# A decoder layer on one core: attention's last value products moved into the next step, and one right-hand operand built one product later

## The chip, the cores and the metric

The kernel runs on one core of one Trainium2 chip. A core has a matrix engine (TensorE, called PE in the profile, with a second row PEld for its weight loads), three engines for elementwise work (VectorE or DVE, ScalarE or ACT, GpSimd or POOL), an engine whose queue here only issues transfers (SyncE or SP), and 16 DMA engines. Each engine takes its instructions in the order in which they stand in its own queue. The metric is the time of one run on the device in microseconds (us). Before the change it is 2248.29 us, the median of 3 runs that lie between 2247.93 and 2248.32 us.

## The reference

One layer for 1024 rows of width 1024, in float32:

```
x = x + 0.5 * swiglu(rms_norm(x), ffn1 weights)            # ffn1, hidden width 2816
h = rms_norm(x)
fq, fk, fv, f_logit, sq, sk, sv, g_fox, g_sb = split(h @ w_in)
y_fox = forgetting_attention(...)     # 8 heads of 64: causal softmax of q.k plus summed log forget gates
y_sb  = stick_breaking_attention(...) # 8 heads of 64: sigmoid(z) times the product of (1 - sigmoid(z)) behind it
x = x + (sigmoid(g_fox) * (y_fox @ w_branch_fox) + sigmoid(g_sb) * (y_sb @ w_branch_sb)) @ w_out
x = x + 0.5 * swiglu(rms_norm(x), ffn2 weights)            # ffn2
x = x + sigmoid(rms_norm(x) @ w_ple_gate) * (p @ w_ple_proj)   # per-layer input embedding, "ple"
```

Here `swiglu(h) = (silu(h @ w_gate) * (h @ w_up)) @ w_down`.

## The kernel before, in words

**Precision.** Every float32 factor is split into two parts that TensorE takes in its faster format: the high part is a rounding copy on ScalarE (a "CAST" row of the profile), the low part is the difference, a subtraction on VectorE (a "TENSOR_TENSOR" row on the same tile). A product is the sum of high by high, high by low and low by high: 12 matmuls of 128x512 for four blocks of the inner dimension.

**The up products.** The gate and up projections of both feed-forward stages, the two gate projections of the mixer and ple's gate projection all go through `make_up`. It computes a 256-column piece n of a weight matrix against the 1024 rows with seven products m = 1 to 7 of sums and differences of quarters instead of eight plain ones. `B[m]` is the right-hand operand of product m, made from the activations; it serves all pieces n of the stage. The last to be made is `B[4]`, in four parts j = 0 to 3: `combo_d(j)` forms the difference on VectorE (two instructions in ffn1, L731 and L732; elsewhere one, L734), and `combo_e(j)` writes its high part (ScalarE, L649) and its low part (VectorE, L653). `begin(s)` issues them behind the s-th product of the stage, in the order of `up_order`: (n, m) = (2,1), (1,5), (2,2), (1,6), (2,6), (1,7), (2,5), (1,3), (2,7), (1,4), and then seven for each further n. So (1,4), the tenth, is the first to read `B[4]`. ffn1 has a form of its own (`rows()`): there its parts are 128 columns of all four inner blocks, so that the first matmul of a product needs all four parts; elsewhere a part is one inner block, and only the fourth matmul of (1,4) needs part 3. `evict` takes a finished product out of its bank; for m = 7 that is a copy on ScalarE, an addition on VectorE and, where n is a gate piece, an activation on ScalarE. The weights are loaded by SyncE's queue into `raw` slots and split by `prep` four products ahead. All of this is issued in exactly the order in which the program writes it.

**Attention.** A step is one head and a quarter c of the rows (256 rows). `scores` makes two rows of blocks (128 rows each) of the scores of a step, one at each resumption; `apply` takes the step before the last, transposes its weights in groups of 256 keys (`transposes`: TensorE into a bank "pt", then a high copy on ScalarE L1212 and a low subtraction on VectorE L1218), and multiplies them with the values (`values`, L1236). `values(0)` is the last product of a step; ScalarE then copies one half of the bank "av" (L1262), and the function `add`, kept in the list `late` until the next `flush`, adds the other half on VectorE (L1265). At the end of a pair of heads `add` also splits y into two parts (ScalarE L1271, VectorE L1272) and sends them to `y_pairs` by two transfers of SyncE. "sc" has three banks, "pt" two and "av" one. `fill` puts projection work of later heads between these pieces. A scheduler sets the order here, but TensorE keeps the written order, and in the stick-breaking heads VectorE and ScalarE keep it too for the operations that are marked with `order`.

**Start and end.** In the first 12 us `busy(count)` issues matmuls whose result nobody reads (L253). At the end, ple's gate (1024 columns in four pieces) is multiplied with a product of p, x is added, and the result is stored. For the last row blocks x is fetched into a tile (`fetch(..., True)`) and added on VectorE; for the first ones x is added by a transfer that accumulates into the tile (L1720, issued by GpSimd). `AT` lists behind which product each of these stands: `fetch` loads, `finish` multiplies and adds, `store` writes a tile out.

Of the kernel before, what the change touches and what calls it, by code (L numbers as in the profile page):

```python
# [18 lines left out]
P = 128  # L19
# [17 lines left out]
def tile_hybrid_decoder_layer(  # L37
# [51 lines left out]
    def f(ap):  # L89
        return ap.bitcast(F32)  # L90
# [434 lines left out]
    def up_order(nm_):  # L525

        seqn = [(2, 1), (1, 5), (2, 2), (1, 6), (2, 6), (1, 7), (2, 5), (1, 3), (2, 7), (1, 4)]
        for n in range(3, nm_ - 1):
            seqn += [(n, 1), (n - 1, 4), (n, 2), (n - 1, 3), (n, 6), (n, 5), (n, 7)]
        n = nm_ - 1  # L530
        return seqn + [(n, 1), (n - 1, 4), (n, 2), (n, 6), (n, 5), (n, 7), (n - 1, 3), (n, 3), (n, 4)]

    def make_up(N, src, nm_, tags, first_fn, first_done=None, over=None):
# [50 lines left out]
        def last_sum(n, eng=nc.gpsimd):  # L584
            eng.tensor_sub(part(n, 2), part(n, 2), part(n, 6))
# [46 lines left out]
        def rows():  # L632
            return "rows" in N[0]
# [108 lines left out]
        def begin(s):  # L742

            if s == 0:
                sums(2, nc.vector, True)
            elif s == 1:
                for q in range(4):
                    combo_s(q, 7)
            elif s == 2:
                last_sum(1, nc.vector)  # L750
            elif s == 3:
                third_sum(2, nc.vector)
            elif s == 7:
                last_sum(2, nc.vector)
            for j in range(4):
                if s == (j + 2 if rows() else 2 + j // 2):
                    combo_d(j)
            if 3 < s < 8:
                combo_e(s - 4)
        return types.SimpleNamespace(a=combo_a, b=combo_b, t=combo_t, l=combo_l, u=combo_u, s=combo_s, load=load, prep=prep, sums=sums, last_sum=last_sum, plain=plain, silu=silu, product=product, begin=begin, E=E, B=B, bank_of=bank_of)  # L760

    def ffn(N, wg, wu, wd, resid, hid, tags, entry, tail):
# [5 lines left out]
        seqn = up_order(nm_)  # L768
# [3 lines left out]
        def evict(n, m, ps):  # L772
            up, j = n % 2, n // 2
            if m == 1:
                E[n] = [slot(t, [P, 2, 512]) for t in (("GF", "RN"), ("Y", "Y"))[up]]
# [348 lines left out]

    def flush():
        while late:
            late.pop(0)()
# [67 lines left out]
    def apply(step, fill):  # L1195
# [3 lines left out]
        av = bank("av")  # L1199
# [23 lines left out]
        def values(kpair):  # L1223
            pt = pts[kpair]
            mm = []
# [32 lines left out]
        values(0)  # L1258
# [3 lines left out]
        nc.scalar.copy(ys, av[HD:P, :256])  # L1262

        def add():
            ins = nc.vector.tensor_add(ys, av[0:HD, :256], ys)  # L1265
            if not step["fox"]:
                order("dve", ins)
            if hh == 1 and c % 2 and not step["last"]:
                cs = slice(c // 2 * 512, c // 2 * 512 + 512)
                hi = slot("PT", [P, 512], F32R)  # L1270
                a = nc.scalar.copy(hi[:], Y["t"][:, cs])  # L1271
                b = nc.vector.tensor_sub(Y["t"][:, cs].bitcast(F32R), Y["t"][:, cs], f(hi[:]))  # L1272
                if not step["fox"]:
                    order("act", a)
                    order("dve", b)
                nc.sync.dma_start(yd[Y["idx"], 0][:, cs], f(hi[:]))
                nc.sync.dma_start(yd[Y["idx"], 1][:, cs], Y["t"][:, cs])
        late.append(add)
# [82 lines left out]
    def attention():  # L1361
# [73 lines left out]
        for h in range(16):  # L1435
# [20 lines left out]
            for c in range(4):  # L1456
# [7 lines left out]
                next(rows)  # L1464
                run(islice(turns, (1, 2, 1, 1)[c]))
# [5 lines left out]
        for step in prev:  # L1471
            run(apply(step, lambda: run(islice(rest, 6))))
        flush()
# [49 lines left out]
    def first_entry(F):  # L1523
# [14 lines left out]
        busy(6)  # L1538
# [12 lines left out]
        busy(4)  # L1551
# [62 lines left out]
    tags = {"raw": {1: ("KH", "KL")}, "sum": {}, "w": ("Q", "Q", "KH", "KL"), "hl": ("WL", "WL", "WL", "WH") + ("PT",) * 4 + ("WL", "WL", "WL", "PT"), "B": {"12": "X", 3: ("T",) * 4, 5: "H", 6: "H", 7: "X", 4: "X"}}  # L1614
# [90 lines left out]
    def ple_start():  # L1705
# [26 lines left out]
        def evict(n, m, ps):  # L1732
# [19 lines left out]
            elif m == 4:  # L1752
# [4 lines left out]
              9: [(fetch, 3, 0, "T")], 10: [(finish, 1, 0)], 11: [(finish, 1, 1), (fetch, 3, 1, "Q"), (store, 0, 0)], 12: [(store, 0, 1), (fetch, 3, 1, "GF", True)],  # L1757
# [61 lines left out]
```

## Time and profile before

| what | value |
|---|---|
| median of 3 runs | 2248.29 us |
| the profiled execution's own time | 2247.58 us |
| span of its trace | 2245.8 us |
| busy: PE, PEld | 2216.0 us (99%), 1881.5 us (84%) |
| busy: DVE, ACT, POOL | 1510.8 us (67%), 1006.0 us (45%), 820.5 us (37%) |
| DMA, mean over the span | 133 GB/s |

The span runs from the first to the last record of the trace; the profiled execution's own time is 1.8 us longer. The busy shares are averages over stages with different limits. The stages, by the lines of their matmuls, lie at: ffn1's entry 0 to 70 us, its up products to 446, its down products to 638, the entry of the gates to 706, gates, values, queries and keys to 850, attention to 1381, branches and output projection to 1500, ffn2's entry to 1567, its up products to 1942 and down products to 2133, ple's entry to 2205, and the end.

### The profile page before, as it was taken

How to read it: one execution, taken by the hardware profiler on the slowest of the kernel's cores; microseconds unless marked ns; L12 is line 12 of the kernel's file. 1: busy time of each engine (PE TensorE's matmuls, PEld its weight loads, DVE VectorE, ACT ScalarE, POOL GpSimd, SP SyncE). 2: the span in 40 equal slices, each digit the busy share in tenths (PEclk: the TensorE clock that was granted, in tenths of full speed). 3: DMA queues.
4: the chain of work that ended last, by engine and by line, in shares of the span. 5: the costliest groups of instructions: out<-in, count | busy, mean ns of one | idle time of the engine just before them, and what ended most of it. 6: DMA issues, size and time to landing. Idle time of an engine off the chain costs nothing.

```text
span 2245.8 us, 30545 instructions
## 1 busy us (share of the span) xinstructions
PE 2216.0 (99%) x11216; PEld 1881.5 (84%) x11216; DVE 1510.8 (67%) x2366; ACT 1006.0 (45%) x1805; POOL 820.5 (37%) x787
## 2 busy tenths in 40 slices
PE   9999999999999999999999999999999999999998
PEld 7788888888888899999898888888888888888886
DVE  8754555598887324666678885889555554778897
ACT  6433333433455435555566663255333333333454
POOL 2353544210021336556566663520544354200111
PEclk9999999999999999999999999999999999999999
DMA  3332323394322334233324466741423232655327
GB/s 132 100 130 80 131 80 131 111 348 168 119 94 97 129 107 129 85 104 86 85 53 100 112 202 214 255 158 49 141 84 128 80 132 80 234 215 192 115 92 225
DMA packets 196183, 298.04 MB, mean 133 GB/s; under 512 B 28729, under 2 KB 108857, under 8 KB 196034
## 3 DMA queue, kind: packets, MB, share of 16 engines
q1 hardware_dynamic: 195312, 293.47, 39.6%
q0 software_dynamic: 720, 2.62, 0.6%
q8 instruction: 88, 1.44, 0.3%
q14 instruction: 61, 0.50, 0.1%
q10 hardware_dynamic: 2, 0.00, 0.0%
HBM read 196.14 MB, written 83.13 MB: 124 GB/s over the span
## 4 chain that ended last, share of the span: by engine, by line
PE 85%; DVE 10%; ACT 2%; issue 1%; DMA 1%; POOL 0%; DVEq 0%; ACTq 0%; POOLq 0%
PE ps L617 37%; PE ps L509 22%; PE ps L895 8%; PE ps L903 5%; PE ps L1498 4%; PE ps L1236 3%; PE ps L1210 2%; PE ps L1152 1%; PE ps L1151 1%; PE ps L561 1%; PE ps L1057 1%; DVE PT L1218 1%; DVE RN L1114 1%; DVE GF L1114 1%; DVE WL L106 1%
## 5 line engine op out<-in xcount | busy, mean ns | idle before, releaser
L509 PE MATMUL ps<-H,H 128*128 128x512 f32 x2184 | 497.3, 389 | 0.0
L509 PEld LDWEIGHTS ps<-H,H 128*128 128x128 f32 x2184 | 409.5, 188 | 84.9
L617 PE MATMUL ps<-H,WL 128*128 128x512 f32 x1176 | 278.3, 389 | 1.5 <-DVE Y L783 0.5
L617 PEld LDWEIGHTS ps<-H,WL 128*128 128x128 f32 x1176 | 220.5, 188 | 48.4 <-DVE Y L783 0.9
L185 POOL TENSOR_TENSOR PT<-PT,PT 128x512 f32<-128x512 f32 x27 | 34.9, 1294 | 403.9 <-ACT PT L182 403.0
L617 PE MATMUL ps<-H,Q 128*128 128x512 f32 x624 | 148.4, 389 | 0.0
L517 DVE SCALAR_TENSOR_TENSOR X<-ps,X 128x512 f32<-128x512 f32 x168 | 110.2, 685 | 47.4 <-PE ps L509 47.3
L617 PE MATMUL ps<-X,WL 128*128 128x512 f32 (+1 forms) x576 | 136.8, 387 | 4.4 <-ACT KH L1780 4.4
L617 PEld LDWEIGHTS ps<-H,Q 128*128 128x128 f32 x624 | 117.1, 188 | 24.3
L617 PEld LDWEIGHTS ps<-X,WL 128*128 128x128 f32 x576 | 107.6, 190 | 26.3 <-ACT KH L1780 4.6
L617 PE MATMUL ps<-H,PT 128*128 128x512 f32 x528 | 125.8, 389 | 0.0
L139 POOL TENSOR_TENSOR WL<-RAW,WH 128x512 fp32r<-128x512 f32 (+1 forms) x84 | 98.6, 1195 | 68.0 <-ACT WH L129 43.6
L1218 DVE TENSOR_TENSOR PT<-ps,PT 128x512 fp32r<-128x512 f32 (+1 forms) x160 | 100.0, 627 | 30.0 <-ACT PT L1212 29.2
L895 PE MATMUL ps<-WH,H 128*128 128x256 f32 x768 | 116.1, 287 | 0.8 <-ACT RN L960 0.8
L617 PEld LDWEIGHTS ps<-H,PT 128*128 128x128 f32 x528 | 99.0, 188 | 20.6
L903 PE MATMUL ps<-H,WH 128*128 128x512 f32 x384 | 115.0, 406 | 0.0
L1236 PE MATMUL ps<-PT,X 128*128 128x256 f32 (+1 forms) x640 | 102.3, 286 | 6.4 <-DVE PT L1218 5.5
L1212 ACT CAST PT<-ps 128x512 fp32r<-128x512 f32 (+1 forms) x160 | 87.1, 548 | 42.5 <-PE ps L1210 41.3
L1236 PEld LDWEIGHTS ps<-PT,X 128*128 128x128 f32 x640 | 90.2, 190 | 16.7 <-DVE PT L1218 10.2
L895 PEld LDWEIGHTS ps<-WH,H 128*128 128x128 f32 x768 | 101.4, 190 | 2.7 <-ACT RN L960 1.3
L412 POOL TENSOR_TENSOR PT<-GF,RN 128x512 f32<-128x512 f32 x20 | 33.7, 1686 | 190.8 <-DVE GF L803 190.8
L1164 POOL TENSOR_TENSOR T<-T,l 128x128 f32<-128x128 f32 (+3 forms) x64 | 73.3, 1148 | 71.8 <-DVE l L1163 69.8
(447 smaller groups left out, 4790.0 us busy)
## 6 DMA issues: line engine op xcount, KB each, us to landing
hidden<-PT SPq DMA_DIRECT2D x40, 512.0 KB, 2.7
WH<-in_ffn_w_gate_dram SPq DMA_DIRECT2D x38, 512.0 KB, 4.7
Q<-hidden SPq DMA_DIRECT2D x24, 512.0 KB, 6.3
hidden<-RN SPq DMA_DIRECT2D x22, 512.0 KB, 2.6
KH<-in_ffn_w_up_dram SPq DMA_DIRECT2D x20, 512.0 KB, 6.2
KL<-in_ffn_w_up_dram SPq DMA_DIRECT2D x20, 512.0 KB, 6.9
T<-in_ffn_w_down_dram SPq DMA_DIRECT2D x20, 512.0 KB, 6.2
GF<-hidden SPq DMA_DIRECT2D x14, 512.0 KB, 7.6
```

Source lines behind the costliest of these rows:

```text
L139: ins = eng_lo.tensor_sub(lo[part], raw[part], f(hi[part]))
L509: pe(nc.tensor.matmul(groups[g][t][:], wt[:, b, k, t * P:(t + 1) * P], act[:, a, k, :], start=(fresh and n == 0), stop=(i in (6, 1, 4) and ...
L517: nc.vector.scalar_tensor_tensor(xs, groups[g][t][:], scale, xs, ALU.mult, ALU.add)
L617: pe(nc.tensor.matmul(ps[:, cols], hl[:, a, k, :], right(B[m], b, k)[:, cols], start=(first and i == 0), stop=(final and i == 11), skip_gr ...
L895: pe(nc.tensor.matmul(ps[:, :n], hT[t // 4](a, k)[:, (t % 4) * P:(t % 4 + 1) * P], w[k // 4][b][:, k % 4, :n], start=(i == 0), stop=(i == ...
L903: pe(nc.tensor.matmul(ps[:], w[a][:, k, :], hT[half](b, k), start=(i == 0), stop=(i == 23)))
L1114: order("dve", nc.vector.tensor_tensor_scan(*args))
L1164: nc.gpsimd.tensor_mul(T[:, :n], T[:, :n], l[:].broadcast_to([P, n]))
L1212: high = nc.scalar.copy(pt[:, 0, :width], ps[:, :width])
L1218: ins = nc.vector.tensor_sub(pt[:, 1, :width], ps[:, :width], f(pt[:, 0, :width]))
L1236: pe(nc.tensor.matmul(o, lh, r, start=(kpair == c and i == 0), stop=(kpair == 0 and i == 3)))
L1498: pe(nc.tensor.matmul(ps[:], w[a][:, k, :], yT[g][b][:, k, half * 512:half * 512 + 512], start=(i == 0), stop=(i == 11)))
```

## The change

Five things are changed.

In attention, `values(0)`, the copy of y and the entry of `add` into `late` become a function `rest`, which is held in the list `held`. The main loop calls it (`settle`) behind the next step's first row of scores, ahead of the next turn of `apply`. `flush` now runs only the calls that were there when it began, and the split and the two transfers of y become a function `parts` that `add` puts into `late`, so that they run one `flush` later. The bank "av" is taken when the first values are written.

In `begin`, `combo_d` and `combo_e` of `B[4]` move: in ffn1 each `combo_d` by one product and each `combo_e` by two, elsewhere `combo_d(2)` and `combo_d(3)` from behind product 3 to behind product 5, and `combo_e(0)` to `combo_e(3)` from behind products 4 to 7 to behind products 5 to 8 (products counted from 0, so that (2,7) is number 8).

In ffn1 alone the first product of piece 3 is put between (2,7) and (1,4), and piece 3 is evicted into two "T" tiles.

At the start, the two later `busy` calls issue 8 and 10 matmuls in place of 6 and 4.

At the end, the fetch of x for the last row block moves from behind product 12, in a "GF" tile, to behind product 9, in a "KL" tile.

```diff
-    def up_order(nm_):
+    def up_order(nm_, rows=False):
         seqn = [(2, 1), (1, 5), (2, 2), (1, 6), (2, 6), (1, 7), (2, 5), (1, 3), (2, 7), (1, 4)]
+        if rows:
+            seqn.insert(-1, (3, 1))
         for n in range(3, nm_ - 1):
-            seqn += [(n, 1), (n - 1, 4), ...
+            seqn += [(n, 1)][rows and n == 3:] + [(n - 1, 4), ...
...
+            d_at, e_at = ((3, 4, 5, 6), (6, 7, 8, 9)) if rows() else ((2, 2, 5, 5), (5, 6, 7, 8))
             for j in range(4):
-                if s == (j + 2 if rows() else 2 + j // 2):
+                if s == d_at[j]:
                     combo_d(j)
-            if 3 < s < 8:
-                combo_e(s - 4)
+            for j in range(4):
+                if s == e_at[j]:
+                    combo_e(j)
...
     def flush():
-        while late:
-            late.pop(0)()
+        for call in [late.pop(0) for _ in late[:]]:
+            call()
+
+    def settle():
+        while held:
+            held.pop(0)()
...
-        values(0)
...
-        nc.scalar.copy(ys, av[HD:P, :256])
         def add():
-            ins = nc.vector.tensor_add(ys, av[0:HD, :256], ys)
+            ins = nc.vector.tensor_add(ys, cell[0][0:HD, :256], ys)
...
             if hh == 1 and c % 2 and not step["last"]:
+                late.append(parts)
...
+        def rest():
+            values(0)
+            nc.scalar.copy(ys, cell[0][HD:P, :256])
+            late.append(add)
+        held.append(rest)
...
                 next(rows)
+                settle()
                 run(islice(turns, (1, 2, 1, 1)[c]))
...
-        busy(6)
+        busy(8)
...
-        busy(4)
+        busy(10)
...
-    tags = {..., "w": ("Q", "Q", "KH", "KL"), "hl": (..., "WL", "WL", "WL", "PT"), ...}
+    tags = {..., "w": ("Q", "Q", "KH", "KL"), "E": {3: ("T", "T")}, "hl": (..., "WL", "WL", "WL", "PT", "WL", "WL", "WL", "WH", "Q", "PT"), ...}
...
-              9: [(fetch, 3, 0, "T")], ... 12: [(store, 0, 1), (fetch, 3, 1, "GF", True)],
+              9: [(fetch, 3, 0, "T"), (fetch, 3, 1, "KL", True)], ... 12: [(store, 0, 1)],
```

Lines of the changed kernel stand two to 23 lines lower than the same lines before: the high part L649 is L651, the low part L653 is L655, the transposes' low part L1218 is L1228, the addition L1265 is L1276 and the split L1272 is L1286.

At the gates' entry, ScalarE's instructions around the end of (2,7), before. The X tile is `B[4]` (L649 writes the high parts from the Q and KH tiles), L1319 and L1321 are the copy and the activation of a product m = 7, L105 the high parts of weights:

```order
L649 CAST X_640_5190<-Q_607_4935 128x512
L105 CAST Q_642_5213<-WH_582_4672 128x512
L649 CAST X_640_5190<-KH_608_4941 128x512
L105 CAST Q_644_5231<-WH_638_5173 128x512
L1326 ACTIVATE GF_611_4971<-GF_611_4971 128x1024
L649 CAST X_640_5190<-KH_609_4947 128x512
L105 CAST PT_645_5252<-RAW_590_4839 128x512
L1319 COPY RN_626_5098<-ps_624_5084 128x512
L1321 ACTIVATE RN_626_5098<-RN_626_5098 128x512
```

The same engine and place after (L1338 and L1340 are the copy and the activation):

```order
L651 CAST X_641_5216<-Q_606_4937 128x512
L105 CAST Q_642_5219<-WH_582_4680 128x512
L651 CAST X_641_5216<-Q_607_4943 128x512
L105 CAST Q_644_5237<-WH_638_5179 128x512
L1345 ACTIVATE GF_611_4979<-GF_611_4979 128x1024
L651 CAST X_641_5216<-KH_608_4949 128x512
L105 CAST PT_645_5258<-RAW_590_4847 128x512
L1338 COPY RN_626_5106<-ps_624_5092 128x512
L1340 ACTIVATE RN_626_5106<-RN_626_5106 128x512
L651 CAST X_641_5216<-KH_609_4955 128x512
```

The high part of part 3 stood ahead of the copy of (2,7) and now stands behind the activation that follows it.

In ffn1, TensorE's instructions around the first reading of `B[4]`, before. X_106_656 is `B[4]`, the T tiles are `B[3]`, X_99_586 is `B[7]`:

```order
L617 MATMUL ps_98_573<-T_55_297,WL_103_634 128x512 x2
L617 MATMUL ps_93_551<-X_99_586,WL_107_659 128x512 x12
L617 MATMUL ps_80_424<-X_106_656,Q_108_681 128x512 x12
L617 MATMUL ps_119_775<-H_5_106,Q_110_699 128x512 x12
L617 MATMUL ps_93_551<-X_106_656,PT_111_720 128x512 x12
```

After, where X_109_700 is `B[4]`:

```order
L619 MATMUL ps_98_581<-T_55_305,WL_103_640 128x512 x2
L619 MATMUL ps_93_559<-X_99_594,WL_106_662 128x512 x12
L619 MATMUL ps_114_752<-H_5_106,WH_107_682 128x512 x12
L619 MATMUL ps_80_432<-X_109_700,Q_110_703 128x512 x12
L619 MATMUL ps_93_559<-X_109_700,PT_111_723 128x512 x12
```

The product of the H tile, (3,1), has changed places with (1,4).

VectorE there, after: the low parts of `B[4]` (L655), the addition of (2,7) (L787), the addition of (1,3) and the multiplication behind it (L791, L807), and the sums of weight piece 3 (L578, L579, L584):

```order
L655 TENSOR_TENSOR X_109_700<-Q_59_309,X_109_700 128x4x128
L106 TENSOR_TENSOR Q_110_703<-KL_15_139,Q_110_703 128x512
L791 TENSOR_TENSOR Y_83_450<-Y_83_450,ps_98_581 128x512
L807 TENSOR_TENSOR GF_65_348<-GF_65_348,Y_83_450 128x1024
L655 TENSOR_TENSOR X_109_700<-Q_62_329,X_109_700 128x4x128
L106 TENSOR_TENSOR PT_111_723<-WH_69_356,PT_111_723 128x512
L787 TENSOR_TENSOR RN_95_573<-RN_95_573,ps_108_685 128x512
L587 TENSOR_TENSOR WH_69_356<-WH_69_356,RAW_96_575 128x4x128
L655 TENSOR_TENSOR X_109_700<-KH_71_372,X_109_700 128x4x128
L578 TENSOR_TENSOR RAW_112_744<-KH_104_643,KL_105_644 128x512
L579 TENSOR_TENSOR RAW_112_744<-RAW_112_744,KH_104_643 128x512
L584 TENSOR_TENSOR KH_104_643<-KH_104_643 128x4x128
```

Three low parts of `B[4]` stand in it, and the last one stands two rows further on. Before, the first three stood ahead of the addition of (1,3) and the last ahead of the addition of (2,7); now two of the four stand behind the addition of (2,7), and the last also behind the sums of piece 3.

In attention, VectorE at the end of a pair of heads (forgetting attention), before. L1218 is the low part of transposed weights, L1265 and L1272 the addition and the split of y, L981 belongs to a projection, L1156 to the scores:

```order
L1218 TENSOR_TENSOR PT_1274_9151<-ps_1273_9146,PT_1274_9151 128x512
L106 TENSOR_TENSOR X_1221_8865<-ps_1264_9103,X_1221_8865 128x4x64
L981 SCALAR_TENSOR_TENSOR KL_1242_8961<-ps_1275_9162,gqk_5955,KH_1241_8960 128x512
L1265 TENSOR_TENSOR Y_1107_8267<-ps_1265_9106,Y_1107_8267 64x256
L1156 ISA T_1279_9191,m_1280_9192<-T_1279_9191,ps_1282_9195 128x128
L1156 ISA m_1280_9192 128x1
L1156 ISA T_1290_9224,m_1291_9225<-GF_1198_8739,ps_1293_9228 128x128
L1156 ISA m_1291_9225 128x1
L981 SCALAR_TENSOR_TENSOR KL_1285_9204<-ps_1286_9205,gqk_5955,KH_1284_9203 128x512
L1272 TENSOR_TENSOR Y_1107_8267<-Y_1107_8267,PT_1278_9186 128x512
L1163 RECIPROCAL l_1281_9193<-l_1281_9193 128x1
L1218 TENSOR_TENSOR PT_1289_9221<-ps_1288_9217,PT_1289_9221 128x384
```

After (L1228 is the low part, L1276 the addition, L1286 the split):

```order
L1228 TENSOR_TENSOR PT_1287_9222<-ps_1286_9218,PT_1287_9222 128x384
L1276 TENSOR_TENSOR Y_1107_8270<-ps_1275_9172,Y_1107_8270 64x256
L1166 ISA T_1289_9231,m_1290_9232<-GF_1198_8742,ps_1292_9235 128x128
L1166 ISA m_1290_9232 128x1
L1166 ISA T_1289_9231,m_1290_9232<-T_1289_9231,ps_1292_9235,m_1290_9232 128x128
L1166 ISA m_1290_9232 128x1
L1286 TENSOR_TENSOR Y_1107_8270<-Y_1107_8270,PT_1288_9226 128x512
L1228 TENSOR_TENSOR PT_1295_9252<-ps_1294_9247,PT_1295_9252 128x512
```

Addition and split now stand behind the first low part of the next turn, and the split ahead of the second.

43 lines of the change are left out of this document (25 added, 18 removed).

## The prediction

> **What bounds the kernel now.** I read the busy shares first, then the stretches of the stages, then what TensorE (PE) waited for.
>
> ```profile
> PE 2216.0 (99%) x11216; PEld 1881.5 (84%) x11216; DVE 1510.8 (67%) x2366; ACT 1006.0 (45%) x1805; POOL 820.5 (37%) x787
> ```
>
> PE is busy 2216.0 of 2245.8 us. No matmul that the output needs is removed, so all that can be gained is PE's idle time, some 30 us, and time at a lower clock. The stretches (length, then busy time of PE, PEld, DVE, ACT, POOL, then PE's granted clock, DMA share and GB/s) say where it lies:
>
> ```profile
> 0.00:70.00 70.00, 64.32 (x285) 48.99 (x286) 60.07 (x97) 45.62 (x90) 12.15 (x22) 1.00 0.34 113
> ...
> 638.00:706.00 68.00, 67.53 (x305) 55.67 (x305) 62.77 (x97) 37.77 (x67) 10.25 (x8) 1.00 0.27 92
> ...
> 850.00:1381.00 531.00, 518.82 (x3497) 472.97 (x3497) 373.06 (x890) 314.27 (x701) 327.75 (x417) 1.00 0.39 110
> ...
> 2205.00:2246.00 41.00, 30.35 (x141) 25.33 (x139) 26.36 (x36) 13.18 (x23) 6.75 (x6) 0.90 0.89 267
> ```
>
> PE idles 5.7 us up to ffn1's first products, 0.5 at the gates' entry, 12.2 in attention and 10.65 in the last 41 us. At the gates' entry DVE is busy 62.77 of 68 us: PE is fed there by a DVE that has almost no slack, and that decides what a later step costs. What PE waited for (total, times, longest):
>
> ```profile
> PE ps L1236 <- DVE PT L1218: 5.5, 13, 1.2
> PE ps L617 <- ACT KH L1780: 4.4, 1, 4.4
> PE ps L1210 <- DVE PT L1218: 4.4, 6, 1.2
> PE ps L617 <- DVE Y L783: 3.0, 2, 2.5
> ...
> PE ps L617 <- DVE RN L1742: 0.5, 1, 0.5
> PE ps L617 <- DVE RN L1320: 0.5, 1, 0.5
> ```
>
> So attention waits 5.5 us for low parts ahead of values and 4.4 us for transposes whose bank a low part must free; the end waits once for 4.4 us; the four entries wait 2.5 us once (ffn1) and 0.5 us three times. Each entry wait is one product waiting for the bank "d" that an addition on DVE has yet to read.
>
> **Gates' entry, and with it ffn2's and ple's.** The rows from (1,3) to the product behind (1,4), with the last high part of `B[4]`:
>
> ```profile
> 705.45 3.02 PE L617 MATMUL ps<-H,WL 128*128 128x512 f32 x12 [0.47 <-DVE RN L1320]
> ...
> 710.70 0.60 ACT L649 CAST X<-KH 128x512 fp32r<-128x512 f32 x1
> ...
> 711.02 2.88 PE L617 MATMUL ps<-X,Q 128*128 128x512 f32 x12
> ...
> 711.73 0.58 ACT L1319 COPY RN<-ps 128x512 f32<-128x512 f32 x1
> ...
> 712.54 0.69 DVE L1320 TENSOR_TENSOR RN<-RN,ps 128x512 f32<-128x512 f32 x1
> ...
> 713.26 0.64 ACT L1321 ACTIVATE RN<-RN 128x512 f32<-128x512 f32 x1 [0.96 <-DVE RN L1320]
> ...
> 713.75 2.88 PE L617 MATMUL ps<-H,Q 128*128 128x512 f32 x12
> ```
>
> (1,4) starts at 711.02 right behind (2,7) and meets its high part, begun at 710.70, in time: no wait. It takes 711.02 to 713.75, 2.73 us or 0.227 us a matmul. After the change that high part stands on ACT behind the copy of (2,7) and the activation that follows it; between these two stands DVE's addition. The gain: two `combo_d` instructions leave DVE ahead of the addition that (1,3) waits for, so the 0.47 us go, and (2,7) ends at 711.02 - 0.47 = 710.55. The loss: from the end of (2,7) to the end of that activation the rows show 711.02 to 713.90, 2.88 us, and the cast adds 0.60, so the high part is there at 710.55 + 3.48 = 714.03. The copy itself waited little there, but DVE now also has to make low parts of `B[4]` ahead of that addition; some 0.9 us (a bit over one instruction of 0.69) brings it to 714.9. (1,4) needs it at its fourth matmul, 710.55 + 3 x 0.227 = 711.23. It stands 3.7 us, does its other nine matmuls in 2.05 and ends at 716.95, against 713.75: **+3.2 us**. The lower end: with no queueing at all the chain is 0.58 + 0.69 + 0.64 + 0.60 = 2.51 us, the high part comes at 713.06, (1,4) ends at 715.1: +1.35; less would need another order of these instructions than the one that is written. The upper end is twice the backlog: +4.1.
>
> A stop of that length also costs clock. The one in ffn1 shows it, below: an idle stretch of 2.5 us is followed by 3.45 us at half clock, worth 1.7 us. The stops of 0.47 us are followed by none. For a stop of 3.7 us I take 1.2 us, between 0 and 1.7, since the start of the slow stretch need not fall into matmuls only. So **+4.4 us** at the gates' entry. ffn2's entry has the same products, the same chain and the same wait of 0.5 us (the second of L783's): **+4.4 us**. ple's has it too, and is settled with the end.
>
> [...]
>
> **ffn1's entry.** Here a matmul needs all four parts, and (3,1) now fills the place ahead of (1,4).
>
> ```profile
> 68.47 0.68 DVE L783 TENSOR_TENSOR Y<-Y,ps 128x512 f32<-128x512 f32 x1
> ...
> 69.21 4.61 PE L617 MATMUL ps<-T,WL 128*128 128x512 f32 x12 [2.48 <-DVE Y L783]
> ...
> 72.37 0.62 ACT L649 CAST X<-KL 128x512 fp32r<-128x512 f32 x1
> 72.44 0.37 SPq L542 DMA_DIRECT2D KL<-in_ffn_w_up_dram  x1
> ...
> 73.65 2.89 PE L617 MATMUL ps<-X,WL 128*128 128x512 f32 x12
> ...
> 81.82 2.43 PE L617 MATMUL ps<-X,PT 128*128 128x512 f32 x10
> ```
>
> ```profile
> 70.20:73.65 3.45, 3.45 (x9) 2.65 (x8) 3.38 (x6) 1.67 (x3) 0.00 (x0) 0.51 0.04 6
> ```
>
> (1,3) waits 2.48 us and then runs 4.44 us at clock 0.51 instead of 2.73: 4.2 us are lost. After the change three DVE instructions of about 0.65 (one `combo_d`, one low part) leave the queue ahead of L783, so (1,3) starts about 67.5, the wait is below 1 us and the clock should hold: (1,3) ends at 70.2, (2,7) at 72.9, (3,1) at 75.7, where before (2,7) ended at 76.4. But DVE's work is only put off. It then has, in order, the third and fourth `combo_d`, a low part, the addition and multiplication of (1,3), another low part, the addition of (2,7), which waits for a copy, and only behind that come ACT's activation, the high part of part 2, a weight cast, the copy of (3,1) and the high part of part 3. The addition of (2,7) ends at about 76.2, and five ACT instructions of about 0.6 bring the last high part to 79.3, where it was done at 73.0. The last low part, needed by the fifth matmul of (1,4), comes behind the sums of piece 3, at about 81.3. So (1,4) starts at 79.3, stands again at 80.2 and ends at 81.3 + 8 x 0.227 = 83.1, or 84.5 if the clock halves. Before, (3,1) and (1,4) were both done at 81.82: +1.3 to +2.7, **taken +2.0**. With the backlog 1.5 us shorter it is +0.0, with the KL weights late (72.44 is their issue now) up to +4.
>
> **ple's entry and the end.** The chain that ended last, then PE's last wait, then two stretches:
>
> ```profile
> 2210.02 7.60 DMA GF<-x_end
> ...
> 2217.63 10.46 DMA out_dram<-GF
> ...
> 2228.11 6.69 DMA GF<-x_end
> ...
> 2234.89 0.69 DVE KH L1722
> ```
>
> ```profile
> 2237.17 2.58 PE L617 MATMUL ps<-X,WL 128*128 128x256 f32 x12 [4.40 <-ACT KH L1780]
> ```
>
> ```profile
> 2205.00:2210.00 5.00, 5.00 (x24) 4.14 (x23) 3.96 (x7) 2.57 (x4) 0.00 (x0) 1.00 0.50 196
> ...
> 2235.00:2240.00 5.00, 2.58 (x12) 2.29 (x12) 4.92 (x7) 1.11 (x3) 0.00 (x0) 0.76 1.03 416
> ```
>
> x for the last block waits for a GF tile that a store must empty: three transfers in a row, 24.75 us. In KL it needs no such tile and is issued behind product 9, where the DMA share is 0.50. So the 4.40 us go from this chain. But ple's entry makes PE 4.4 us later, by the reckoning above, and then the last products themselves end at the old time. Two limits remain: if ple's entry costs only 1.35 us, DMA (share 1.03 at the very end) still has the same stores to send, and I allow a gain of 1.5; if it costs 4.4 and the last half product also restarts slowly, +3. **Taken 0** for both together. On SP's queue the moved load goes ahead of a load of p and of two stores of GF and RN; its KL tile was last read by the sums of an earlier piece, so I see no wait for it there.
>
> **The start.**
>
> ```profile
> 1.32 2.74 PE ps L253 x6
> 4.06 3.76 PE ps L239 x4
> ```
>
> Two and six more of the idle matmuls at 0.457 us are 0.9 and 2.7 us. PE idles there anyway, part of the 5.7 us. If they only run on, as slow as these, past the point where the next real work is ready, I bound the loss by +1.0; if they bring the clock up earlier, the gain by -0.8, half of what a slow stretch cost in ffn1. Taken 0.
>
> **Attention.** One pair of heads' end, one late stick-breaking step, and the wait on DVE for the copy of y:
>
> ```profile
> 1047.86 0.62 PE L1236 MATMUL ps<-PT,X 128*128 128x256 f32 x3 [0.34 <-DVE PT L1218]
> ...
> 1048.92 0.42 DVE L1265 TENSOR_TENSOR Y<-ps,Y 64x256 f32<-64x256 f32 x1
> ...
> 1050.59 0.68 DVE L1272 TENSOR_TENSOR Y<-Y,PT 128x512 fp32r<-128x512 f32 x1
> ...
> 1051.95 0.63 PE L1210 MATMUL ps<-identf,T 128*128 128x128 f32 x4 [0.64 <-DVE PT L1218]
> ...
> 1253.63 0.62 PE L1236 MATMUL ps<-PT,X 128*128 128x256 f32 x3 [1.19 <-DVE PT L1218]
> ```
>
> ```profile
> DVE Y L1265 <- ACT Y L1262: 32.0, 32, 2.3
> ```
>
> The first row is `values(0)` waiting for its low part; held behind a row of scores it should not wait. The fourth is a transpose whose bank is freed late because addition and split of y stand ahead of the first low part; now they stand behind it. Going through the single waits by their place, I put the first kind at 3.8 of the 5.5 us and the second at 3 of the 4.4. The last is `values(1)` waiting behind DVE's scans in a late stick-breaking step; nothing moves away from it but DVE's own waits for the copy of y. Against that, the addition (0.42 us) and the split (0.69) now come behind the first low part, where DVE's low parts are what PE waits for: 0.4 us in each of the 8 long stick-breaking steps is 3.2. So -3.8 - 3 + 3.2 = -3.6, and with some of the 32.0 us of DVE's idle time used **-5 us**; from -12.2 (all idle time of the stretch) to +3 (no wait removed, each addition in the way).
>
> **The sum.** 0 + 2.0 + 4.4 + 4.4 + 0 - 5 = +5.8 us on the profiled 2247.58: 2253.4. The median of the runs stands 0.7 us above the profiled execution, so **2254 us**.
>
> **Rivals.** (a) DVE's idle 32.0 us are what attention lacks: freed of the wait for the copy, DVE is early with every low part and all 12.2 us of PE's waits go. Then the sum is 0 + 2 + 8.8 - 12.2 = -1.4, **2247 us**, not slower than before; it decides from a gain of 10.8 on. For it speaks that 9.9 of the 12.2 us name L1218, against it that the largest of them (1.19 at 1253.63) stand in the middle of a turn. (b) The held products cost what they save, because the additions meet the low parts: attention +3 to 0, **2259 to 2262 us**. For it speaks 373.06 us of DVE work there with waits on its low parts; against it that DVE is busy only 70% of that stretch. (c) The entries stop only as long as the bare chain: 1.35 us each at gates and ffn2, no half clock (a stop of 1.8 us), ffn1 0, ple and end -1.5: 0 + 0 + 2.7 - 1.5 - 5 = -3.8, **2244.5 us**. Against it speaks that DVE is busy 62.77 of 68 us there.
>
> **Chances.** The forecast's family (entries stop, attention gains some) 0.50, reaching from 2249 to 2258; (b) 0.22; (a) 0.18; (c) 0.10. A measurement of this kernel can tell about 0.2%, 4.5 us, from no change: same is 2243.8 to 2252.8. Slower: 0.37 of the first and all of (b), 0.59; same: 0.13, 0.10 of (a), 0.07 of (c), 0.30; faster: 0.08 where (a) meets short entry stops, and 0.03 of (c), 0.11. The range that leaves out 2 in 10 is 2246 to 2263; the forecast's own is 2249 to 2258.
>
> **What would show it.** At the gates, ffn2 and ple the wait of 0.5 us ahead of (1,3) gone, and a new one of 2 to 4.5 us inside (1,4), PE waiting for an ACT cast into X (L651), with a clock near 0.5 behind it. In ffn1 (1,3) without its 2.48 us and a stop of 3 to 4 us ahead of (1,4). In attention, fewer waits on L1228. At the end no wait of 4.4 us on the activation. If X's casts do not appear among PE's waits, the forecast is wrong.

## The result, and the profile after

The changed kernel takes 2269.7 us, the median of 4 runs (2268.85 to 2270.72); the kernel before, run beside it, takes 2248.31 us (2247.93 to 2248.85). The ratio is 1.0095, with a 95% interval of 1.0078 to 1.0113: slower by 21.4 us. The forecast had the sign, but with 2254 us less than a third of the loss, and the time lies outside its range.

The profile after, in the page's busy shares and in the list of what PE waited for (total, times, longest):

```profile
PE 2225.4 (98%) x11224; PEld 1888.9 (83%) x11224; DVE 1514.7 (67%) x2366; ACT 1008.9 (44%) x1805; POOL 825.2 (36%) x787
```

```profile
PE ps L619 <- ACT X L651: 15.6, 5, 4.7
PE ps L1249 <- DVE PT L1228: 8.2, 13, 1.3
PE ps L1220 <- DVE PT L1228: 3.8, 4, 1.4
PE ps L997 <- DVE X L106: 2.3, 2, 1.9
...
PE ps L619 <- DVE Y L787: 0.6, 1, 0.6
PE ps L619 <- ACT KH L1803: 0.5, 1, 0.5
```

Two things stand in these lines. A wait that did not exist before, PE on ScalarE's casts into X (the high parts of `B[4]`), takes 15.6 us in five pieces, and it is the largest. The waits that were to go have gone: L787 has 0.6 us where L783 had 3.0, the activation at the end 0.5 us where it had 4.4. But PE is also 9.4 us longer *busy*, with the same products and a few idle matmuls more. That is mostly the clock: in or behind the new stops the granted clock (the number behind POOL's bracket) is half. The first row is the stop in ffn1; the others are the slow stretches from edge to edge, with PE's busy time as the second number.

```profile
77.58:80.99 3.41, 0.02 (x1) 0.02 (x1) 2.77 (x6) 2.73 (x6) 0.00 (x0) 1.00 0.97 294
80.99:87.82 6.83, 6.56 (x15) 4.69 (x16) 4.63 (x7) 1.07 (x2) 5.01 (x4) 0.50 0.16 55
719.28:726.11 6.83, 5.64 (x13) 4.46 (x14) 3.45 (x6) 2.76 (x5) 1.28 (x1) 0.50 0.01 2
1060.62:1064.03 3.41, 3.41 (x19) 3.41 (x18) 2.27 (x6) 1.76 (x6) 1.24 (x2) 0.50 0.66 154
1589.68:1596.51 6.83, 4.18 (x10) 3.32 (x11) 4.61 (x8) 2.18 (x4) 0.84 (x1) 0.50 0.09 32
2231.39:2234.80 3.41, 2.92 (x7) 2.37 (x8) 2.91 (x5) 0.95 (x2) 0.30 (x1) 0.50 0.94 217
```

The one at 1060.62 lies in attention, in the forgetting heads. It stands behind a new stop there, PE waiting for the low part of a projection (L106):

```profile
1060.10 0.66 PE L997 MATMUL ps<-identf,RN 128*128 128x128 f32 x4 [1.92 <-DVE X L106]
```

The time by stages, from the start of the same matmul in the two traces (a matmul that ends one stage and begins the next):

| up to | before | after | later by | this stage | forecast |
|---|---|---|---|---|---|
| ffn1's first up product | 31.05 | 32.43 | 1.4 | +1.4 | 0 (start) |
| first down product of ffn1 | 446.30 | 451.84 | 5.5 | +4.2 | +2.0 |
| first product behind the gates | 776.30 | 787.84 | 11.5 | +6.0 | +4.4 |
| last value product of attention | 1380.85 | 1396.36 | 15.5 | +4.0 | -5 |
| first down product of ffn2 | 1941.96 | 1963.65 | 21.7 | +6.2 | +4.4 |
| end of the span | 2245.8 | 2268.5 | 22.7 | +1.0 | 0 (ple and end) |

At the gates, the rows that answer to those shown of before, in the timeline after:

```profile
715.80 0.61 PE L619 MATMUL ps<-X,Q 128*128 128x512 f32 x2
716.73 0.60 ACT L651 CAST X<-KH 128x512 fp32r<-128x512 f32 x1
...
717.38 0.50 PE L619 MATMUL ps<-X,Q 128*128 128x512 f32 x1 [0.97 <-ACT X L651]
717.75 0.58 ACT L1338 COPY RN<-ps 128x512 f32<-128x512 f32 x1
...
718.57 0.68 DVE L1339 TENSOR_TENSOR RN<-RN,ps 128x512 f32<-128x512 f32 x1
719.28 0.63 ACT L1340 ACTIVATE RN<-RN 128x512 f32<-128x512 f32 x1 [0.95 <-DVE RN L1339]
719.82 0.60 ACT L651 CAST X<-KH 128x512 fp32r<-128x512 f32 x1
...
720.47 3.78 PE L619 MATMUL ps<-X,Q 128*128 128x512 f32 x8 [2.59 <-ACT X L651]
```

It is the chain that was foretold: copy, addition, activation, cast, and PE's fourth matmul behind it. Part 2's cast is late as well, behind the wide activation (L1345), and takes 0.97 us of the stop. And in ffn1:

```profile
68.66 3.06 PE L619 MATMUL ps<-T,WL 128*128 128x512 f32 x12 [0.55 <-DVE Y L787]
71.55 2.88 PE L619 MATMUL ps<-X,WL 128*128 128x512 f32 x12
74.27 2.88 PE L619 MATMUL ps<-H,WH 128*128 128x512 f32 x12
80.97 2.08 PE L619 MATMUL ps<-X,Q 128*128 128x512 f32 x4 [3.82 <-ACT X L651]
83.31 3.78 PE L619 MATMUL ps<-X,Q 128*128 128x512 f32 x8 [0.27 <-DVE X L655]
```

(1,3) has lost most of its wait, and (1,4), the row at 80.97, has got a longer one, with a second short one for the last low part.

### The profile page after: what moved, and what is told of

The parts are those of the page before. It is cut to its first block, busy times and chain, and to the rows that moved or that the text cites. A ratio compares the mean times of both kernels' runs of the same rounds, so it can differ in the third digit from the quotient of the medians.

```text
span 2268.5 us, 30594 instructions
## 1 busy us (share of the span) xinstructions
PE 2225.4 (98%) x11224; PEld 1888.9 (83%) x11224; DVE 1514.7 (67%) x2366; ACT 1008.9 (44%) x1805; POOL 825.2 (36%) x787
## 4 chain that ended last, share of the span: by engine, by line
PE 83%; DVE 9%; ACT 3%; issue 1%; POOL 1%; DMA 1%; SPq 0%; DVEq 0%; ACTq 0%; POOLq 0%
PE ps L619 37%; PE ps L509 22%; PE ps L899 7%; PE ps L907 4%; PE ps L1521 3%; PE ps L1249 2%; PE ps L563 2%; PE ps L1220 2%; PE ps L1162 1%; PE ps L1161 1%; PE ps L1061 1%; DVE PT L1228 1%; DVE RN L1118 1%; DVE GF L1118 1%; DMA RAW<-x_end 1%
## 5 line engine op out<-in xcount | busy, mean ns | idle before, releaser
L1228 DVE TENSOR_TENSOR PT<-ps,PT 128x512 fp32r<-128x512 f32 (+1 forms) x160 | 100.0, 629 | 47.0 <-ACT PT L1222 44.4
L619 PE MATMUL ps<-X,Q 128*128 128x512 f32 x372 | 96.9, 410 | 12.4 <-ACT X L651 12.1
L1249 PEld LDWEIGHTS ps<-PT,X 128*128 128x128 f32 x640 | 90.4, 190 | 16.9 <-DVE PT L1228 11.0
L619 PEld LDWEIGHTS ps<-X,Q 128*128 128x128 f32 x372 | 73.5, 199 | 30.1 <-ACT X L651 13.7
```

Of the source, the lines that this page charges most:

```text
L619: pe(nc.tensor.matmul(ps[:, cols], hl[:, a, k, :], right(B[m], b, k)[:, cols], start=(first and i == 0), stop=(final and i == 11), skip_gr ...
L1228: ins = nc.vector.tensor_sub(pt[:, 1, :width], ps[:, :width], f(pt[:, 0, :width]))
L1249: pe(nc.tensor.matmul(o, lh, r, start=(kpair == c and i == 0), stop=(kpair == 0 and i == 3)))
```

## The experiments

Each run stands beside runs of the kernel before on the same chip, whose medians were 2247.59, 2248.16 and 2247.77 us in the three sets; the ratios are what is to be compared.

**Each part alone.** First the change in attention (the diff of `apply`, `flush`, `settle` and the main loop, nothing else).

> The kernel before with the change in attention alone (values(0), the copy and the addition of y held back, the split of y one flush later). Theory from the trace of the whole change: attention itself loses 4.0 us, whatever the entries do, because in the stick-breaking steps the addition now stands between two low parts on VectorE; the time is 2252.3 (2250.5 to 2254). Rival, the forecast's term: attention alone gains some 5 us, and what was lost in it came from the shifted entries; the time is 2243 (2236 to 2247).

Measured: 2251.29 us, ratio 1.0017 (1.0008 to 1.0027), +3.7. Attention itself loses, about what it lost in the whole change's trace (4.0), so the shifted entries are not the cause. By the waits from 1195 us to the end of attention, which is about the last six of the eight stick-breaking heads, in this run and in the kernel before:

```profile
PE ps L1245 <- DVE PT L1224: 6.2, 8, 1.3
PE ps L1216 <- DVE PT L1224: 0.5, 1, 0.5
```

```profile
PE ps L1236 <- DVE PT L1218: 4.4, 9, 1.2
```

The later parts of `B[4]` at the gates, ffn2 and ple:

```diff
-                if s == (j + 2 if rows() else 2 + j // 2):
+                if s == ((2, 3, 4, 5) if rows() else (2, 2, 5, 5))[j]:
                     combo_d(j)
...
+                if s == ((4, 5, 6, 7) if rows() else (5, 6, 7, 8))[j]:
+                    combo_e(j)
```

> The kernel before with the differences and high and low parts of B[4] moved at the entries of the gates, ffn2 and ple alone, ffn1 as before. Theory: PE stops 3.4 to 4.7 us ahead of the fourth matmul of (1,4) at each, and runs at half clock behind it; gates +6.0, ffn2 +6.2 as in the whole change, ple about +5, of which up to 4.4 vanish in the wait that the end has anyway; the time is 2261 to 2263. Rival, the forecast's price (stop 3.2, half clock 1.2 each): 2257 to 2258. Rival, the bare chain: 2251.

Measured: 2259.55 us, ratio 1.0055 (1.0040 to 1.0070), +12.0: more than half of the whole loss. It has the stops of the whole change, 0.97 and 2.59 us at the gates and 4.75 at ffn2. It is 1.5 us below what was expected: at the gates 3.41 us then ran at clock 0.50, where the whole change has a slow stretch of 6.83. The late entry of ple costs almost nothing here: PE's last wait, 4.4 us before, falls to 0.5 us by it, and from the first down product of ffn2 to the end of the span the run takes 0.6 us longer than the kernel before.

ffn1's entry alone (`up_order` with (3,1) ahead of (1,4), the later `combo_d` and `combo_e` there, the T tiles and, as in the whole change, one subtraction for weight piece 2, `last_sum(2)`, behind product 8 in place of 7).

> The kernel before with ffn1's entry alone changed: (3,1) ahead of (1,4), the parts of B[4] later there, piece 3 in T tiles. Theory: as in the whole change, +4.2, the time 2252.5 (2251 to 2254): the stop of 2.5 us goes, one of 3.8 us comes, and half clock lasts longer behind it. Rival, the forecast's term: +2.0, 2250.3.

Measured: 2251.41 us, ratio 1.0016 (1.0007 to 1.0025), +3.8.

The end alone (the fetch moved from behind product 12 to behind product 9, into KL).

> The kernel before with the earlier fetch of x for the last row block alone. Theory A: the chain of three transfers is what PE waits 4.4 us for; without it and without a late entry ahead, PE ends about 4 us earlier, and the stores leave a gain of 1.2 to 4: 2244 to 2247. Theory B: the DMA engines are full to the end, and the last store lands when it did: 2248.3, within 0.5.

Measured: 2248.31 us, ratio 1.0003 (0.9993 to 1.0012): no difference. PE's wait did fall, from 4.40 to 0.47 us, and its last half product began 3.1 us earlier. But the chain that ended last found another way to the same end:

```profile
2215.58 9.83 DMA RN<-x_end
2225.82 11.24 DMA RAW<-p_proj
2237.15 1.24 DVE Y L1718
```

The loads of p and x for another block (RAW) stand in SyncE's queue behind a store of RN, which waits for the accumulation into RN. The load that was moved now runs beside that accumulation, and RAW takes 11.24 us. VectorE's last additions start at 2237.15, when they started at 2236.19 before. The time is that of theory B, and the DMA share is 1.01 or more in each 5 us from 2215 to 2240; that a shorter list of transfers would end sooner was not tried.

The idle matmuls at the start alone (8 and 10).

> The kernel before with the longer runs of idle matmuls at the start alone. Theory from the trace of the whole change, where the first up product started 1.4 us later: the added matmuls run at half clock and push the first transposes, +1.4, 2249.6 (2248.8 to 2250.2). Rival: the clock rises earlier and pays for them, or the start differs by as much from one execution to the next: 2248.2, within 0.6.

Measured: 2248.45 us, ratio 1.0003 (0.9994 to 1.0012): the rival. In its trace the ten idle matmuls of the second set take 2.33 us, in the whole change's 4.37; ffn1's first up product starts at 30.87, against 31.05 before and 32.43 in the whole change. The 11 runs spread over 4.1 us, those of the kernel before over 2.4, so a slow start in some of them is not ruled out. The parts alone sum to 3.7 + 12.0 + 3.8 + 0.7 + 0.7 = 20.9 us; the whole is 21.4. That leaves no sign that they act on each other, though the intervals are 4 to 7 us wide.

**Why the entries stop.** The last part was put one product earlier (the third stays behind product 7), so that it stands ahead of the copy of (2,7) in ScalarE's queue; all else is as in the run of the entries alone:

```diff
-            ... (5, 6, 7, 8)
+            ... (5, 6, 7, 7)
```

> The kernel before with the parts of B[4] moved at the gates, ffn2 and ple as in the change, but with the last two high and low parts one product earlier, behind product 7, so that they stand ahead of the copy of (2,7) on ScalarE. Theory: the stop ahead of the fourth matmul of (1,4) hangs on that one place in ScalarE's queue; it vanishes, and the half clock with it, and the waits of 0.5 us ahead of (1,3) are gone too: 2246.5 to 2248.5. Rival: the parts are late because VectorE is full there, wherever they stand; a stop of 1 us or more stays in each entry and the time is 2251 or more.

Measured: 2250.55 us, ratio 1.0009 (1.0000 to 1.0018). One product earlier for this one part (its cast on ScalarE and its low part on VectorE) is worth 9.6 of the 12.0 us. But not all: in this run PE still waits,

```profile
711.47 1.73 PE L617 MATMUL ps<-X,Q 128*128 128x512 f32 x5 [0.97 <-ACT X L649]
```

```profile
1575.55 3.11 PE L617 MATMUL ps<-X,Q 128*128 128x512 f32 x6 [1.66 <-DVE X L653]
```

for part 2's cast at the gates and for a low part on VectorE at ffn2. So theory and rival each hold a piece. With the second and third part one product earlier too, only the differences and the first part were left where the change puts them:

```diff
-            ... (5, 6, 7, 7)
+            ... (5, 5, 6, 7)
```

> The kernel before with the differences of B[4] at the gates, ffn2 and ple where the change puts them (the last two behind product 5), the first two high and low parts there too, and the last two behind products 6 and 7 as before. Theory: no part stands behind (2,7), the addition that (1,3) waits for comes earlier, and no stop is left: -0.5 in two entries, ple's hidden by the wait at the end: 2246.5 to 2248. Rival, from the run with the last two parts behind product 7: VectorE is full, the two differences that were put off make the third part late by themselves, a stop of about 1 us stays at the gates and up to 1.7 at ffn2: 2249.5 to 2251.

Measured: 2246.81 us, ratio 0.9996 (0.9987 to 1.0005). The stops are gone but for 0.68 us at ffn2, and so are the waits ahead of (1,3). The later differences are not what costs; the later high and low parts of parts 1 to 3 are.

**What the half clock costs.** Twelve matmuls that nobody reads were put into the stop, so that PE is not idle:

```diff
+            if (n, m) == (1, 4) and not rows():
+                spare = bank("av")
+                for q in range(12):
+                    pe(nc.tensor.matmul(spare[:], hl[:, 0, q % 4, :], right(B[7], 0, q % 4), start=True, stop=True))
```

> The kernel before with the later parts of B[4] at the gates, ffn2 and ple as in the change, and 12 matmuls ahead of (1,4) whose result is not read; they add nothing that is computed and take 2.7 us of the stop. It measures the half clock. Theory: the stops still end when the cast of the last high part ends, but the clock stays up, so only the half clock's cost goes: by the matmuls that ran slow in the whole change 12 and 8 in the two entries at 0.2 us, 2.4 and 1.6, and with ple's about 5: 2254.5 to 2256.5 against 2259.5. Rival, the forecast's 1.2 each: 2257.

Measured: 2256.77 us, ratio 1.0040 (1.0027 to 1.0054). The rest of the stop is still there, and the clock behind it is full:

```profile
714.54 2.33 PE L621 MATMUL ps<-X,Q 128*128 128x512 f32 x9 [1.12 <-ACT X L653]
```

```profile
714.50:716.00 1.50, 1.46 (x6) 1.24 (x7) 1.45 (x3) 0.51 (x1) 0.00 (x0) 1.00 0.00 0
716.00:719.00 3.00, 3.00 (x15) 2.46 (x14) 2.69 (x4) 1.10 (x2) 1.18 (x1) 1.00 0.25 93
```

In the run without the fill, 715.88 to 719.30 had clock 0.50. By the medians the half clock is worth 12.0 - 8.6 = 3.4 us, though each of the two intervals is some 6 us wide. The stages of the two traces say where: with the fill the gates take 1.6 us less and the up products of ffn2 2.1 us less. ple's entry has nothing to give, since its lateness falls into PE's last wait. So it is some 1.8 us for each of two entries, not 1.2 for each of three; that the time came out at the rival's 2257 is luck.

**ffn1, with the parts left where they were.**

```diff
+        if rows:
+            seqn.insert(-1, (3, 1))
...
-                if s == (j + 2 if rows() else 2 + j // 2):
+                if s == ((3, 4, 5, 6) if rows() else (2, 2, 3, 3))[j]:
                     combo_d(j)
             if 3 < s < 8:
                 combo_e(s - 4)
```

> The kernel before with ffn1's entry changed as to the order ((3,1) ahead of (1,4), T tiles, the differences one product later) but the high and low parts of B[4] left where they were. Theory: the loss of 3.8 us comes from the parts being put behind the addition of (2,7); left ahead, they are ready for (1,4), while two instructions less stand ahead of the addition that (1,3) waits for; its wait of 2.5 us falls to about 1.3, and with it the half clock: 2244 to 2246. Rival: VectorE's work is the same in sum, the parts are late again: 2248 or more.

Measured: 2245.43 us, ratio 0.9987 (0.9978 to 0.9996), -2.7. (1,3) waits half as long, the clock holds, and (1,4) waits for nothing:

```profile
68.15 3.03 PE L619 MATMUL ps<-T,WL 128*128 128x512 f32 x12 [1.20 <-DVE Y L787]
```

```profile
68.15:72.00 3.85, 3.85 (x17) 3.18 (x18) 3.78 (x7) 1.14 (x2) 0.00 (x0) 1.00 0.00 0
```

**Attention, with the addition ahead of the first low part.**

```diff
         def turn_and_scan(kpair):
...
-            low()
             flush()
+            low()
             fill()
```

> The kernel before with the change in attention, but with the flush ahead of the low part in each turn, so that the addition of y comes before the first low part again, as it was. Theory: the addition behind the first low part is what costs in the stick-breaking steps; ahead of it, it fills time in which VectorE waits for ScalarE's cast: the stick-breaking steps lose nothing, the drain at the end still 1: 2248 to 2249.5, against 2251.3. Rival: the loss comes from the row of scores that now stands between values(1) and values(0), and the time stays at 2251 to 2252.

Measured: 2247.28 us, ratio 0.9996 (0.9988 to 1.0005): the loss of 3.7 us is gone, and the rest cannot be told from no change. (The exchange moves all that `flush` calls: the addition and, at the end of a pair of heads, the split.) VectorE's rows of one stick-breaking step show it, first with the addition behind the first low part (attention alone), then ahead of it; the last row of each is `values(1)` of that step on PE:

```profile
1311.76 0.56 DVE L1224 TENSOR_TENSOR PT<-ps,PT 128x384 fp32r<-128x384 f32 x1 [2.03 <-ACT PT L1218]
1312.35 0.42 DVE L1272 TENSOR_TENSOR Y<-ps,Y 64x256 f32<-64x256 f32 x1
...
1313.14 0.67 DVE L1224 TENSOR_TENSOR PT<-ps,PT 128x512 fp32r<-128x512 f32 x1
...
1316.72 0.62 PE L1245 MATMUL ps<-PT,X 128*128 128x256 f32 x3 [1.08 <-DVE PT L1224]
```

```profile
1309.36 0.42 DVE L1272 TENSOR_TENSOR Y<-ps,Y 64x256 f32<-64x256 f32 x1 [1.27 <-ACT Y L1291]
1309.86 0.56 DVE L1224 TENSOR_TENSOR PT<-ps,PT 128x384 fp32r<-128x384 f32 x1
...
1310.66 0.67 DVE L1224 TENSOR_TENSOR PT<-ps,PT 128x512 fp32r<-128x512 f32 x1
...
1314.29 0.62 PE L1245 MATMUL ps<-PT,X 128*128 128x256 f32 x3 [0.37 <-DVE PT L1224]
```

From the first low part to the second are 1.38 us in the one and 0.80 in the other. Ahead of the first low part VectorE waits for ScalarE's cast anyway; the addition costs nothing there. The waits for low parts ahead of values fall, over the same stretch as above (from 1195 us on), to

```profile
PE ps L1245 <- DVE PT L1224: 3.2, 5, 1.6
```

from 6.2 us.

**What is worth keeping.** ffn1's order with its parts left in place, and the addition first:

> ffn1's entry as in the run that gained there ((3,1) ahead of (1,4), differences one product later, high and low parts where they were) and attention's held products with the addition ahead of the first low part; all else as before. Theory: the two lie in separate stages and add up, -2.7 and -0.9: 2244 to 2245.3. Rival: attention's gain was noise: 2245.4.

Measured: 2243.2 us, ratio 0.9980 (0.9972 to 0.9989), -4.6, 1 us more than the two gains added up. And with the later differences at the other entries:

> The same, and the parts of B[4] at the gates, ffn2 and ple as in the run of this set that moves them alone. Theory: whatever that one changes is added: 2243.5 to 2244.5 if its stops are gone, 2246 to 2247 if VectorE is full there.

Measured: 2241.77 us, ratio 0.9974 (0.9963 to 0.9984), -6.0: faster than both kernels, and the best of all that was run. It is 1.7 us below the lower of the two forecasts, and why was not looked into; its lead over the run before it is within the intervals.

## Why the prediction was right or wrong

The trace of the whole change is 16.9 us longer than the forecast's sum makes it: 9.0 of them are attention's, 3.4 those of the gates and ffn2, 2.2 ffn1's, 1.4 the start's and 1.0 the end's.

**Gates, ffn2: the mechanism was right, and the stop's size at the gates too.** The forecast put the end of the last cast at 714.9. It ended at 720.42 in a trace that was 5.54 us late at that place: 714.88. The stop of 3.7 us measured 0.97 + 2.59. In part that is luck. The 0.9 us for VectorE's low parts were put ahead of the addition of (2,7); they came one addition earlier, ahead of that of (1,3), which the wide activation on ScalarE waits for, so that the copy of (2,7) started late. At ffn2 the stop was 4.75 us, and there "the same chain" was misread: between the end of the copy (1587.64) and the addition (1590.43) VectorE has a wide multiplication, a sum, a low part of `B[4]` and one of the weights to do; at the gates only the last stands there. One price for both was too low. What was mis-sized beside it is the half clock: 1.2 us a stop by the forecast. In this trace 5.64 and 4.18 us of matmuls lie in the slow stretches, so 2.8 and 2.1 us were lost. With them the stages come out: -0.5 + 3.6 + 2.8 = 5.9 against 6.0 measured at the gates, -0.5 + 4.8 + 2.1 = 6.4 against 6.2 at ffn2. I took the 1.7 us that the slow stretch behind ffn1's wait takes from its matmuls, in the one trace of before, for the most that one can cost; here the stretch of 6.83 us in ffn1 took 3.3 (6.56 us of matmuls in it).

**ffn1: the same.** The wait ahead of (1,3) was to fall below 1 us and is 0.55. The high part was to come at 79.3; it comes at 80.9 in a trace that is 1.4 us late, 79.5. I let the clock halve only for part of (1,4) and took the middle, +2.0; it was halved from 80.99 to 87.82, 3.3 us lost, and the stage lost 4.2. What the slow stretch cost before was read too high as well. In the run with only the differences later the clock held behind the same wait (1.00 from 69.38 to 76.00), and the fifth matmul of (1,4) still begins 7.5 us behind the first of (1,3), against 8.1 before, since (1,4) then waits 0.87 us for the last low part.

**Attention: the step that failed.** "So -3.8 - 3 + 3.2 = -3.6, and with some of the 32.0 us of DVE's idle time used -5 us." Measured: +4.0, and +3.7 alone. What rival (b), at 0.22, describes is what happened in attention, and its +3 to 0 was still too little.

The first term, -3.8 us for the waits of `values(0)`, failed by a misreading. Of PE's waits ahead of values (those over 0.1 us, gone through by their place in the step) only 2.1 us stand ahead of `values(0)`, most of them in the forgetting heads; 4.2 us stand ahead of `values(1)`, nearly all in the stick-breaking heads. Holding `values(0)` back removed nearly all of the first kind (0.6 us is left in attention alone), but the second kind grew to 7.8 us, because the addition now delays the low parts behind it. With the two lines exchanged it is back at 4.2.

The second term held and was used up. The transposes' waits up to 1195 us did go down, from 4.4 to 1.6 us. But a new stop came, of PE on a low part of a projection (L997, the row of 1.92 us above), with 3.41 us at half clock behind it. So the forgetting heads, from the first product behind the gates to the first scores of the ninth head, take 334.2 us where they took 334.5. In the first run of what is worth keeping, whose profiled execution had a mean granted clock of 0.999 against 0.993 in the whole change's, they take 332.2. Why the scheduler puts that low part late was not tried.

The third term, 3.2 us for the addition in the stick-breaking heads, has the right cause. From the first scores of the ninth head to the last value product they take 269.8 us before, 272.6 in attention alone, 274.1 in the whole change, and 269.9 with the addition first. The forecast set against it waits that are not there in those heads. The idle 32.0 us of VectorE ahead of the addition were not lost time either: VectorE was waiting there for a cast all the same, as the exchange of two lines shows. In the whole change's trace 1.5 us of the loss lie in the last two steps, where no scores follow; that piece varies by 0.8 us in the traces where attention is unchanged, and what lengthens it was not tried apart.

**The end: right by luck.** Taken 0, measured 0 alone and +1.0 with the entries. The forecast let the earlier fetch pay for ple's late entry. Neither is there: the earlier fetch gains nothing by itself, although PE's wait goes, since the last additions wait for another load; and without it ple's late entry costs 0.6 us, since it falls into PE's last wait.

**The start** was taken 0 and is 0 when run alone, by the median; the +1.4 us of the whole change's trace go with idle matmuls that ran slow in that execution. Of the 5.7 us of idle time that the forecast counted on there, 2.5 are ffn1's wait, so only 3.2 lie at the start.

**The rivals.** (a), 2247 us, and (c), 2244.5 us, did not come about. The range ended at 2263 since I added (b) to the likeliest entries, and not to the longer stops and stretches at half clock that the upper ends of the same terms allowed (+4.1 and 1.7 at each of two entries, +4 in ffn1, +1 at the start, +3 at the end, +3 in attention: 2271).

## What to carry to other kernels

When work is put later to relieve one wait, look at what then stands ahead of it in each queue: here a cast that had been free stood behind an eviction that waits for the matrix engine, and the matrix engine waited for the cast (2.59 us at the gates, 4.75 at ffn2). An operation can be free in one place of an engine's queue and cost its whole length one place on, if the engine idles at the first place for a reason of its own; here an addition of 0.42 us put two low parts 1.38 us apart in place of 0.80, and the exchange of two lines was worth 4.6 us (+3.7 against -0.9). Before a wait is counted as a gain, look which product of the step it stands ahead of. And the upper ends of several terms that can go wrong the same way should be added up, not averaged.

## What the runs showed of the hardware

In the traces of before and of the whole change, every stretch at half clock that begins behind 13 us and ends before the last matmul lasts 3.41 or 6.83 us: 70.17 to 73.58 before, and the five that are shown with the profile after. The starts of these five lie 187, 100, 155 and 188 times 3.413 us apart. The length of a stop alone does not tell whether the clock falls. Behind the same wait of 2.5 us in ffn1 it was half for 3.41 us in the trace of before:

```profile
66.75:70.17 3.42, 0.96 (x4) 0.83 (x5) 3.39 (x6) 1.14 (x2) 0.00 (x0) 1.00 0.00 0
70.17:73.58 3.41, 3.41 (x9) 2.65 (x9) 3.38 (x6) 1.67 (x3) 0.00 (x0) 0.50 0.02 4
```

In the run with only the differences later it was 1.00 throughout:

```profile
69.38 3.02 PE L617 MATMUL ps<-T,WL 128*128 128x512 f32 x12 [2.50 <-DVE Y L785]
```

```profile
66.90:69.38 2.48, 0.01 (x1) 0.01 (x1) 2.44 (x5) 1.14 (x2) 0.00 (x0) 1.00 0.00 0
69.38:73.00 3.62, 3.62 (x16) 3.00 (x17) 3.58 (x6) 0.99 (x2) 0.00 (x0) 1.00 0.00 0
73.00:76.00 3.00, 3.00 (x14) 2.17 (x12) 2.96 (x5) 1.26 (x3) 0.00 (x0) 1.00 0.63 174
```

What sets the two apart was not shown. In the 3.41 us ahead of the slow stretch PE was busy for 0.96 us before, and for 0.02 to 1.49 us ahead of the five of the whole change; behind 1.78 us of work in one such length there, 2258.69 to 2262.10, the next 3.42 us had clock 1.00:

```profile
77.58:80.99 3.41, 0.02 (x1) 0.02 (x1) 2.77 (x6) 2.73 (x6) 0.00 (x0) 1.00 0.97 294
715.87:719.28 3.41, 1.04 (x4) 0.30 (x2) 2.35 (x4) 2.46 (x4) 0.00 (x0) 1.00 0.38 154
1057.21:1060.62 3.41, 1.49 (x15) 1.36 (x14) 2.47 (x10) 2.43 (x6) 1.29 (x2) 1.00 0.39 155
1586.27:1589.68 3.41, 1.31 (x6) 0.75 (x4) 3.38 (x5) 1.37 (x3) 0.00 (x0) 1.00 0.05 17
2227.98:2231.39 3.41, 0.47 (x3) 0.04 (x1) 2.67 (x4) 1.32 (x4) 0.76 (x1) 1.00 0.53 211
2258.69:2262.10 3.41, 1.78 (x13) 1.48 (x12) 2.71 (x4) 0.82 (x3) 0.00 (x0) 1.00 1.03 418
2262.10:2265.52 3.42, 0.00 (x0) 0.00 (x0) 2.04 (x5) 0.00 (x0) 0.00 (x0) 1.00 1.02 408
```

Behind a stop of 1.66 us at ffn2 (shown above, last part one product earlier) six matmuls took 3.11 us; behind one of 2.02 us at the same place in the run with the filled stop nine took 2.33:

```profile
1579.69 2.33 PE L621 MATMUL ps<-X,Q 128*128 128x512 f32 x9 [2.02 <-ACT X L653]
```
